# When the weight difference for S7 is taken, and who reads A11's sum first

## The chip, the cores and the metric

The kernel runs on one core of a Trainium2 chip. The metric is the device time of one execution in microseconds (us), the median of several runs. The engines are TensorE (PE, its weight loads PEld), VectorE (DVE), ScalarE (ACT), GpSimd (POOL) and SyncE (SP), which issues the DMA transfers here. They run at their own pace and wait for each other through semaphores; each works through its own queue in order.

## What is computed

Two layers of a transformer-like backbone run on 128 context tokens and 512 latent tokens at once (640 columns), with the same weights. Each layer is: a modulated RMSNorm and a half-step SwiGLU FFN, a token-mixing stage, and a second such FFN. The change touches the FFNs alone:

```python
D_MODEL = 1024; D_FF = 2816; DEPTH = 2; SEQ = 128; DEC_SEQ = 512

def swiglu(h, wi, wo):
    a, b = jnp.split(h @ wi, 2, axis=-1)
    return (jax.nn.silu(a) * b) @ wo

def trunk_layer(x, mod, ...):
    h = mod_norm(x, norm_g[0], mod, 0)
    x = x + 0.5 * mod[..., 2, :] * swiglu(h, ffn1_wi, ffn1_wo)
    ...                                # token mixing
    h = mod_norm(x, norm_g[2], mod, 2)
    x = x + 0.5 * mod[..., 8, :] * swiglu(h, ffn2_wi, ffn2_wo)
```

All is float32. The modulation `mod` (adaLN) is a product of the conditioning with its own weights; the kernel computes it in short bursts on TensorE between other work.

## The kernel before

**Precision.** A float32 product is made of three passes. Weights and data are each split into a high part (rounded to the format TensorE takes, `fp32r`) and a low part (what is left); the passes are high x high, low x high and high x low. The weights come as raw float32 tiles by DMA. For each weight block ScalarE writes the high part (line 256, `wt<-raw`) and GpSimd the low part (line 257, which reads the raw block and the high part). I call the two together a conversion; they are made by `w_split`, one block after the other in the order of a list that `ffn_convs` writes out.

**Seven products for eight.** The first product of an FFN, `h @ wi`, is cut into 22 blocks of 128 columns of `a` and of `b`. For one block the weights are two raw tiles of 128x1024, each seen as two halves of 128x512: `r[0]` holds A11 and A12, `r[1]` holds A21 and A22. The 640 tokens are cut in two halves of 320. The 2x2 product of blocks is made with seven products instead of eight (the scheme of Strassen and Winograd). Each is 12 matmuls of 128x320. Their order in a block, with the weights, and the bank of PSUM that each adds to, is

- S2 (A21+A22, bank D), S5 (A11+A12, bank C), A22 (bank D again), A11 (bank C again), S1 (A11+A22, bank A), S6 (A21-A11, bank E), S7 (A12-A22, bank A again).

The data operands are named B (for S2 and S5), X (A22 and S1), P (A11, S7) and Q (S6 and the last pass of S7). So in the views one product is a row `ps<-X,wt x12`, and S7 is a row of 8 with P and one of 4 with Q; A11 is the row with P x12.

**Sums and differences of weights.** They are VectorE operations of 128x512, all recorded on line 121 (`into`). Each is the `prep` of an entry of the list: `s2` writes the sum for S2 to `sq`; `s5` writes the sum for S5 to `acc` and calls `s7`, the difference for S7, which is written in place (`raw<-raw`); `s6`, the difference for S6, also in place, belongs to A22; `s1` writes the sum for S1 to `t`. `w_split` takes the prep of the next entry as soon as it has issued a conversion, and an entry whose prep was issued in one step of the program (`self.now`, one per product) is converted in a later step at the earliest. An entry without a prep may follow at once. Which step is reached when, and so the place of every conversion among the other instructions, is thus set by the list, by the number of weight slots that are free (`wcap`) and by the calls of `pump` after each product.

**What is done with the products.** `step` reads the banks. After S2, ScalarE copies bank D to `b` (line 844). After S5, VectorE adds bank C to it (line 851). After A22, `gate_a` reads bank D and `b` (line 869). After A11, ScalarE takes the silu of bank C into the first half of `a` (line 859), and VectorE adds bank C to the first half of `b` or subtracts (line 860). Line 860 also adds bank A to `b` after S1 and bank E after S6. After S6 the first halves of `a` and `b` are multiplied (line 821); after S7 VectorE adds bank A to the second half of `a` (line 855), ScalarE takes its silu (line 856), VectorE multiplies the second halves (line 821 again), and the result is split in a high and a low part `av` (lines 828 and 829).

**Stages of an FFN.** The first four blocks are written out by hand in `first`, product by product across blocks, with their own list entries. Then the groups of `FFG` follow (4, 2, 4, 4, 4, 4 blocks; the first of these is `first`): the blocks of a group one after the other, then the part of the second product, `(...) @ wo`, that this group feeds (lines 443, 445, 447, read by line 672). Conversions for later blocks go on all the while. In some groups of the first three FFNs an adaLN burst (line 368) stands between A22 and A11.

Of the kernel before, what the change touches and what calls it, by code (L numbers as in the profile page):

```python
# [81 lines left out]
class Kernel:  # L82
# [26 lines left out]
    def ffn_convs(self, f, u0):  # L109


        nc = self.nc
        out = []

        def conv(name, j, units, src, prep=None, frees=()):
            out.append(Conv((f, name, j), units, src, prep, frees, early=name != "D" and j >= FIRST))

        q = lambda r, i: r[:, i * 512 : i * 512 + 512]

        def into(o, x, y, op=ALU.add, eng=nc.vector):  # L120
            eng.tensor_tensor(o, x, y, op=op)  # L121

        ab = lambda j: (u0 + 2 * j, u0 + 2 * j + 1)
        first = range(FIRST)
        for j in first:
            b = ab(j)[1]
            conv("S2", j, (b,), lambda r: q(r[0], 0), lambda r: into(q(r[0], 0), q(r[0], 0), q(r[0], 1)))
            conv("A22", j, (b,), lambda r: q(r[0], 1), frees=(b,))
        for j in first:
            a = ab(j)[0]  # L130
            conv("S5", j, (a,), lambda r: q(r[0], 1), lambda r: into(q(r[0], 1), q(r[0], 0), q(r[0], 1)))
            conv("A11", j, (a,), lambda r: q(r[0], 0), frees=(a,))

        def s6(r, eng=nc.vector):
            into(q(r[1], 0), q(r[1], 0), q(r[0], 0), ALU.subtract, eng)

        def s7(r, eng=nc.vector):
            into(q(r[0], 1), q(r[0], 1), q(r[1], 1), ALU.subtract, eng)

        def s2(r):  # L140
            assert not self.acc_live
            into(self.nb["sq"][:, :512], q(r[1], 0), q(r[1], 1))

        def s5(r):
            into(self.nb["acc"][:, :512], q(r[0], 0), q(r[0], 1))
            s7(r)

        def s1(r):
            into(self.nb["t"][:, :512], q(r[0], 0), q(r[1], 1))

        j0, ud = 0, u0 + 2 * NFF
        for name, j in ((name, j) for j in first for name in ("S1", "S7", "S6")):
            a, b = ab(j)
            if name == "S1":
                eng = nc.gpsimd if f == (0, 0) and ("S1", j) in ON_POOL else nc.vector
                conv("S1", j, (a, b), lambda r: q(r[0], 0), (
                    lambda r, eng=eng: s6(r, eng), lambda r, eng=eng: s7(r, eng),
                    lambda r, eng=eng: into(q(r[0], 0), q(r[0], 0), q(r[1], 1), eng=eng),
                ))
            elif name == "S7":  # L160
                conv("S7", j, (a,), lambda r: q(r[0], 1), frees=(a,))
            else:
                conv("S6", j, (b,), lambda r: q(r[0], 0), frees=(b,))
        for gi, gn in enumerate(FFG):
            for j in range(max(j0, FIRST), j0 + gn):
                a, b = ab(j)
                conv("S2", j, (a, b), lambda r: self.nb["sq"][:, :512], s2)
                conv("S5", j, (a, b), lambda r: self.nb["acc"][:, :512], s5)
                conv("A22", j, (a, b), lambda r: q(r[1], 1), s6)
                conv("A11", j, (a, b), lambda r: q(r[0], 0))  # L170
                conv("S1", j, (a, b), lambda r: self.nb["t"][:, :512], s1)
                conv("S6", j, (a, b), lambda r: q(r[1], 0), frees=(b,))
                conv("S7", j, (a,), lambda r: q(r[0], 1), frees=(a,))
            for i in range(gn * KD // 8):
                for h in range(2):
                    conv("D", (gi, 2 * i + h), (ud,), lambda r, h=h: q(r[0], h), frees=(ud,) if h else ())
                ud += 1
            j0 += gn
        return out
# [613 lines left out]
    def ffn(self, l, s, gate, nxt):  # L793
# [7 lines left out]
        half = [slice(*self.geo.half[g]) for g in range(2)]  # L801
        tt, add, sub, mul = nc.vector.tensor_tensor, ALU.add, ALU.subtract, ALU.mult
# [33 lines left out]
        def step(p, name, now=None, pump=99):  # L836


            self.now += 1
            x, acc, start = USE[name]  # L840
            bank = p[acc]
            self.prod((f, name, p["j"]), x, bank, start)
            if name == "S2":
                nc.scalar.copy(p["b"][:, half[0]], bank)
            elif name == "A22":
                if p["early"]:
                    nc.scalar.copy(p["b"][:, half[1]], bank)
                else:
                    gate_a(p)
            elif name == "S5":  # L850
                tt(p["b"][:, half[0]], p["b"][:, half[0]], bank, op=add)
                if p["early"]:
                    gate_a(p)
            elif name == "S7":
                tt(p["a"][:, half[1]], p["a"][:, half[1]], bank, op=add)
                nc.scalar.activation(p["a"][:, half[1]], p["a"][:, half[1]], AF.Silu)
            else:
                if name == "A11":
                    nc.scalar.activation(p["a"][:, half[0]], bank, AF.Silu)  # L859
                tt(p["b"][:, half[0]], bank, p["b"][:, half[0]], op=sub if p["neg"] else add)  # L860
                p["neg"] = False
            if now is not None:
                now()
            self.ada_rest()
            if pump:
                self.pump(n=pump)

        def gate_a(p):
            tt(p["a"][:, half[1]], p["D"], p["b"][:, half[0]], op=sub)

        def new(j):
            a, b = (self.tp.tile([128, PADW], F32, name=n, tag="t" + n)[:, :NT] for n in "ab")
            return {"j": j, "neg": True, "early": j < FIRST, "a": a, "b": b}

        def first():
# [6 lines left out]
            def st(name, j, now=None, pump=0):  # L882
                if name == "S2":
                    banks(ps[j], "DC")
                elif name in ("S1", "S6"):
                    banks(ps[j], "A" if name == "S1" else "E")
                step(ps[j], name, now, pump)
# [131 lines left out]
        for gi, gn in enumerate(FFG):  # L1019
            pairs = first() if gi == 0 else None  # L1020
            for j in range(FIRST if gi == 0 else j0, j0 + gn):
                p = new(j)
                if s and j == NFF - 2:
                    self.ada_stop = True
                banks(p, "CE")
                banks(p, "DA")
                step(p, "S2")
                end(1)
                step(p, "S5")
                end()  # L1030
                step(p, "A22")
                self.ada_tick()
                step(p, "A11")
                step(p, "S1")
                if l == s == 0:
                    self.ada_tick()
                step(p, "S6", lambda: gated(p, 0))
                if pairs is None:
                    pairs = av(gn)
                step(p, "S7", lambda: finish(p, pairs[j - j0]))  # L1040
# [993 lines left out]
```

## Time and profile before

| what | us |
|---|---|
| median of 3 runs | 2570.98 |
| lowest and highest run | 2566.62, 2575.92 |
| the profiled execution | 2573.96 |
| its span, first to last instruction | 2572.2 |
| TensorE busy in the span | 2378.7 |
| GpSimd busy | 1546.1 |
| VectorE busy | 1695.7 |
| ScalarE busy | 1037.5 |

The profile is one execution. Its page gives the busy time of each engine, the chain of work that ended last (followed back from the last instruction, at each step to what released it) and the costliest groups of instructions. The trace behind it answers narrower questions: who waited for whom, and the instructions of one engine in order of time in a window. In the timeline a row gives start and duration in us, engine, line, operation, output and inputs, a count of merged instructions, and in brackets the idle time of the engine ahead of it with what ended it. Matmuls overlap at their edges, so a product of 12 has a row of 1.92 us although the next starts 1.76 us after it. Times count from the start of the span.

### The profile page before, as it was taken

The page shows a single profiled execution, that of the slowest core. Times are in us where ns is not written, and L with a number is a line of the kernel's source. Part 1 is how long each engine was busy: PE and PEld are TensorE (multiplying, and loading weights), DVE is VectorE, ACT ScalarE, POOL GpSimd, SP SyncE. Part 2 cuts the span into 40 slices and gives each one's busy share as a digit, 9 for nine tenths or more (in the row PEclk, how much of TensorE's full clock was granted, in tenths as well). Part 3 has the DMA queues.
Part 4 walks back from the last instruction along what each step waited for, and adds up shares of the span by engine and source line. Part 5 has one row for each costly group of instructions (what it writes and reads, how often), then busy time and mean ns, then how long its engine had stood idle before and what let it go on. Part 6 is the DMA issues. An engine that isn't in the chain of part 4 may idle for free.

```text
span 2572.2 us, 45355 instructions
## 1 busy us (share of the span) xinstructions
PE 2378.7 (92%) x17790; PEld 2314.6 (90%) x17790; DVE 1695.7 (66%) x2931; ACT 1037.5 (40%) x2234; POOL 1546.1 (60%) x1460
## 2 busy tenths in 40 slices
PE   5699999989889899999997999999889898999999
PEld 4698999989888899999996999999889798999999
DVE  6466566667675876556666776666766767766664
ACT  5233233333664533233343333334437654343332
POOL 2565567653366575565564876667434676677663
PEclk9799999989999999999998999999989999999999
DMA  7465422231112234556231321224111032222121
GB/s 268 143 239 201 158 89 83 82 95 56 31 39 99 82 115 179 210 202 216 92 119 60 105 75 66 82 83 124 40 54 44 31 126 99 82 83 91 58 82 50
DMA packets 80484, 272.31 MB, mean 106 GB/s; under 512 B 9232, under 2 KB 15120, under 8 KB 80272
## 3 DMA queue, kind: packets, MB, share of 16 engines
q1 hardware_dynamic: 79408, 269.33, 30.8%
q8 instruction: 140, 2.29, 0.4%
q14 instruction: 72, 0.59, 0.1%
q10 hardware_dynamic: 864, 0.10, 0.0%
HBM read 265.73 MB, written 3.67 MB: 105 GB/s over the span
## 4 chain that ended last, share of the span: by engine, by line
PE 68%; DVE 16%; issue 5%; ACT 4%; POOL 4%; DMA 2%; SPq 0%; POOLq 0%; ACTq 0%; DVEq 0%
PE ps L787 29%; PE ps L443 9%; PE ps L445 9%; PE ps L447 9%; DVE raw L121 3%; PE ada L368 2%; POOL wt L257 2%; DVE acc L121 1%; DVE b L860 1%; DVE t L121 1%; PE qk L1262 1%; PE qk L1263 1%; PE qk L1261 1%; POOL win L1115 1%; DMA raw<-in_w 1%
## 5 line engine op out<-in xcount | busy, mean ns | idle before, releaser
L257 POOL TENSOR_TENSOR wt<-raw,wt 128x512 fp32r<-128x512 f32 (+1 forms) x562 | 902.2, 1622 | 501.8 <-ACT wt L256 500.8
L443 PE MATMUL ps<-av,wt 128*128 128x320 f32 (+2 forms) x1536 | 477.7, 312 | 0.1
L447 PE MATMUL ps<-av,wt 128*128 128x320 f32 (+2 forms) x1536 | 474.2, 310 | 0.0
L256 ACT ACTIVATE wt<-raw 128x512 fp32r<-128x512 f32 (+1 forms) x562 | 350.7, 659 | 294.2 <-issue 149.1
L445 PE MATMUL ps<-av,wt 128*128 128x320 f32 (+2 forms) x1536 | 460.4, 311 | 0.0
L672 DVE SCALAR_TENSOR_TENSOR x<-ps,modv,x 128x512 f32<-128x512 f32 (+3 forms) x496 | 231.5, 512 | 267.4 <-PE ps L447 198.7
L787 PE MATMUL ps<-X,wt 128*128 128x320 f32 x2112 | 346.1, 314 | 28.4 <-DVE b L860 8.1
L787 PE MATMUL ps<-B,wt 128*128 128x320 f32 x2112 | 339.9, 317 | 32.7 <-POOL wt L257 13.1
L787 PEld LDWEIGHTS ps<-B,wt 128*128 128x128 f32 x2112 | 323.7, 194 | 38.2 <-POOL wt L257 16.0
L787 PEld LDWEIGHTS ps<-X,wt 128*128 128x128 f32 x2112 | 319.0, 190 | 35.9 <-DVE b L860 8.3
L787 PE MATMUL ps<-P,wt 128*128 128x320 f32 x1760 | 298.1, 318 | 30.7 <-DVE b L860 24.5
L787 PEld LDWEIGHTS ps<-P,wt 128*128 128x128 f32 x1760 | 269.6, 193 | 44.4 <-DVE b L860 25.0
L443 PEld LDWEIGHTS ps<-av,wt 128*128 128x128 f32 x1536 | 290.4, 189 | 1.9 <-issue 0.8
L447 PEld LDWEIGHTS ps<-av,wt 128*128 128x128 f32 x1536 | 290.1, 189 | 0.0
L445 PEld LDWEIGHTS ps<-av,wt 128*128 128x128 f32 x1536 | 285.8, 189 | 1.6 <-issue 1.4
L860 DVE TENSOR_TENSOR b<-ps,b 128x320 f32<-128x320 f32 x240 | 116.8, 487 | 201.8 <-ACT a L859 129.7
L787 PE MATMUL ps<-Q,wt 128*128 128x320 f32 x1408 | 237.5, 312 | 0.0
L121 DVE TENSOR_TENSOR raw<-raw 128x512 f32<-128x512 f32 x181 | 208.2, 1155 | 13.8 <-DMA raw<-in_w 8.7
L787 PEld LDWEIGHTS ps<-Q,wt 128*128 128x128 f32 x1408 | 216.6, 190 | 0.2 <-DVE t L821 0.2
L257 POOL TENSOR_TENSOR wt<-t,wt 128x512 fp32r<-128x512 f32 x72 | 93.7, 1301 | 130.6 <-ACT wt L256 92.7
L257 POOL TENSOR_TENSOR wt<-acc,wt 128x512 fp32r<-128x512 f32 x72 | 112.9, 1569 | 64.9 <-ACT wt L256 64.9
L257 POOL TENSOR_TENSOR wt<-sq,wt 128x512 fp32r<-128x512 f32 x72 | 112.3, 1560 | 60.4 <-ACT wt L256 60.4
(275 smaller groups left out, 4027.4 us busy)
## 6 DMA issues: line engine op xcount, KB each, us to landing
raw<-in_w SPq DMA_DIRECT2D x311, 512.0 KB, 3.5
ada<-in_adat SPq DMA_DIRECT2D x40, 1024.0 KB, 7.5
ada<-in_adat SPq DMA_DIRECT2D x64, 512.0 KB, 6.5
scraw<-in_w SPq DMA_DIRECT2D x33, 512.0 KB, 3.8
x<-in_xt SPq DMA_DIRECT2D x2, 1280.0 KB, 7.8
out_yt<-x SPq DMA_DIRECT2D x16, 160.0 KB, 1.8
dft<-in_dft SPq DMA_DIRECT2D x4, 512.0 KB, 4.0
kqv<-in_inv SPq DMA_DIRECT2D x4, 336.0 KB, 4.5
```

What stands on the lines that cost most here:

```text
L121: eng.tensor_tensor(o, x, y, op=op)
L256: nc.scalar.activation(hi, src, AF.Copy)
L257: nc.gpsimd.tensor_tensor(lo, src, hi.bitcast(F32), op=ALU.subtract)
L368: nc.tensor.matmul(ps[32 * q : 32 * q + 32, 0, :128], self.scP[:, k, :], units[q // parts][:, k * 128 : k * 128 + 128], start=(i == 0), st ...
L443: mm(out, w[0], x[0], start=start, stop=False)
L445: mm(out, w[0], x[1], start=False, stop=part == 1 and stop)
L447: mm(out, w[1], x[0], start=False, stop=part is None and stop)
L672: self.nc.vector.scalar_tensor_tensor(out=self.x[:, d, c0:c1], in0=ps[:, c0 - o : c1 - o], scalar=self.mod(l, s, d, cond), in1=self.x[:, d ...
L787: mm(out, w[:, k * 128 : k * 128 + 128], v[:, k * 320 : k * 320 + 320], start=start and i == k == 0, stop=i == 2 and k == 3, skip_group_ch ...
L860: tt(p["b"][:, half[0]], bank, p["b"][:, half[0]], op=sub if p["neg"] else add)
L1115: steps.append(lambda: nc.gpsimd.tensor_tensor(out(), a(), b(), op=op))
L1261: mm(ps[:, 0, :256], h0, wk[:, 0, :], start=(k == 0), stop=False)
```

## The change

It has two parts. The difference for S7 is no longer taken with the prep of S5 but becomes the prep of A11, in the list for blocks from the fifth on. And in `step`, for A11, the instruction of VectorE that adds bank C to `b` stands ahead of ScalarE's silu of the same bank; this part holds for the first four blocks of each FFN too.

```diff
         def s5(r):
             into(self.nb["acc"][:, :512], q(r[0], 0), q(r[0], 1))
-            s7(r)
...
-                conv("A11", j, (a, b), lambda r: q(r[0], 0))
+                conv("A11", j, (a, b), lambda r: q(r[0], 0), s7)
...
             else:
+                tt(p["b"][:, half[0]], bank, p["b"][:, half[0]], op=sub if p["neg"] else add)
+                p["neg"] = False
                 if name == "A11":
                     nc.scalar.activation(p["a"][:, half[0]], bank, AF.Silu)
-                tt(p["b"][:, half[0]], bank, p["b"][:, half[0]], op=sub if p["neg"] else add)
-                p["neg"] = False
```

In the changed file lines from 146 on count one less; line 860 has become 857, and line 859 has become 860. The number of instructions is the same on every engine, and TensorE, GpSimd and SyncE have the same instructions in the same order.

VectorE, the end of the first block of a group of four and the start of the second, before (`t<-raw` is the sum for S1):

```order
L860 TENSOR_TENSOR b<-ps,b 128x320
L821 TENSOR_TENSOR b<-a,b 128x320
L121 TENSOR_TENSOR t<-raw 128x512
L855 TENSOR_TENSOR a<-a,ps 128x320
L821 TENSOR_TENSOR b<-a,ps 128x320
L851 TENSOR_TENSOR b<-b,ps 128x320
L829 TENSOR_TENSOR av<-b,av 128x640
```

and now:

```order
L857 TENSOR_TENSOR b<-ps,b 128x320
L820 TENSOR_TENSOR b<-a,b 128x320
L121 TENSOR_TENSOR raw<-raw 128x512
L854 TENSOR_TENSOR a<-a,ps 128x320
L820 TENSOR_TENSOR b<-a,ps 128x320
L121 TENSOR_TENSOR t<-raw 128x512
L850 TENSOR_TENSOR b<-b,ps 128x320
L828 TENSOR_TENSOR av<-b,av 128x640
```

The difference (`raw<-raw`) has taken the place of `t` ahead of S7's sum (line 855, now 854), and `t` has gone behind the product of the second halves, ahead of the next block's sum for S5 (line 851, now 850).

VectorE, the second block of that group, from the high and low split of the first block's result (line 829) on, before:

```order
L829 TENSOR_TENSOR av<-b,av 128x640
L869 TENSOR_TENSOR a<-ps,b 128x320
L121 TENSOR_TENSOR sq<-raw 128x512
L860 TENSOR_TENSOR b<-ps,b 128x320
L121 TENSOR_TENSOR acc<-raw 128x512
L121 TENSOR_TENSOR raw<-raw 128x512
L860 TENSOR_TENSOR b<-ps,b 128x320
L121 TENSOR_TENSOR raw<-raw 128x512
L860 TENSOR_TENSOR b<-ps,b 128x320
L821 TENSOR_TENSOR b<-a,b 128x320
L855 TENSOR_TENSOR a<-a,ps 128x320
L821 TENSOR_TENSOR b<-a,ps 128x320
```

and now:

```order
L828 TENSOR_TENSOR av<-b,av 128x640
L868 TENSOR_TENSOR a<-ps,b 128x320
L121 TENSOR_TENSOR sq<-raw 128x512
L857 TENSOR_TENSOR b<-ps,b 128x320
L121 TENSOR_TENSOR acc<-raw 128x512
L857 TENSOR_TENSOR b<-ps,b 128x320
L121 TENSOR_TENSOR raw<-raw 128x512
L857 TENSOR_TENSOR b<-ps,b 128x320
L820 TENSOR_TENSOR b<-a,b 128x320
L121 TENSOR_TENSOR raw<-raw 128x512
L854 TENSOR_TENSOR a<-a,ps 128x320
L820 TENSOR_TENSOR b<-a,ps 128x320
```

Behind `acc` one difference is gone, so that S1's sum follows it; the difference now stands behind the product of the first halves (line 821, now 820), ahead of S7's sum (line 855, now 854).

ScalarE, the same turn from the first to the second block, from the silu of A11 on, before (`wt<-...` are high parts of weights):

```order
L859 ACTIVATE a<-ps 128x320
L256 ACTIVATE wt<-sq 128x512
L256 ACTIVATE wt<-acc 128x512
L256 ACTIVATE wt<-raw 128x512 x2
L856 ACTIVATE a<-a 128x320
L844 COPY b<-ps 128x320
L256 ACTIVATE wt<-t 128x512
L256 ACTIVATE wt<-raw 128x512
```

and now:

```order
L860 ACTIVATE a<-ps 128x320
L255 ACTIVATE wt<-sq 128x512
L255 ACTIVATE wt<-acc 128x512
L255 ACTIVATE wt<-raw 128x512
L855 ACTIVATE a<-a 128x320
L255 ACTIVATE wt<-raw 128x512
L843 COPY b<-ps 128x320
L255 ACTIVATE wt<-t 128x512
L255 ACTIVATE wt<-raw 128x512
```

The last conversion of the four, that of A11, has moved from ahead of S7's silu (line 856, now 855) to behind it, and so ahead of the copy of S2's bank (line 844, now 843).

## Rows read from the trace of the kernel before

**Rows 1.** The page: busy time and share of each engine; the chain by engine.

```profile
PE 2378.7 (92%) x17790; PEld 2314.6 (90%) x17790; DVE 1695.7 (66%) x2931; ACT 1037.5 (40%) x2234; POOL 1546.1 (60%) x1460
...
PE 68%; DVE 16%; issue 5%; ACT 4%; POOL 4%; DMA 2%; SPq 0%; POOLq 0%; ACTq 0%; DVEq 0%
```

**Rows 2.** Waits of TensorE and VectorE: who for whom, us in total, times, longest.

```profile
PE ps L787 <- DVE b L860: 32.6, 35, 8.1
...
PE ps L787 <- DVE t L860: 6.2, 3, 2.5
...
PE ps L787 <- DVE a L869: 4.5, 3, 1.5
...
DVE b L860 <- ACT a L859: 129.7, 63, 7.9
```

**Rows 3.** Timeline of TensorE in a plain group of four blocks.

```profile
1579.94 1.92 PE L787 MATMUL ps<-X,wt 128*128 128x320 f32 x12
1581.70 1.92 PE L787 MATMUL ps<-P,wt 128*128 128x320 f32 x12
...
1587.37 1.43 PE L787 MATMUL ps<-P,wt 128*128 128x320 f32 x8 [0.23 <-DVE b L860]
...
1593.10 2.02 PE L787 MATMUL ps<-X,wt 128*128 128x320 f32 x12 [0.18 <-ACT b L844]
...
1601.20 1.45 PE L787 MATMUL ps<-P,wt 128*128 128x320 f32 x8 [0.81 <-DVE b L860]
...
1606.60 1.92 PE L787 MATMUL ps<-X,wt 128*128 128x320 f32 x12
```

**Rows 4.** Timeline of VectorE in the same group.

```profile
1584.13 0.49 DVE L860 TENSOR_TENSOR b<-ps,b 128x320 f32<-128x320 f32 x1 [1.74 <-ACT a L859]
...
1585.26 1.66 DVE L121 TENSOR_TENSOR raw<-raw 128x512 f32<-128x512 f32 x1
1586.84 0.48 DVE L860 TENSOR_TENSOR b<-ps,b 128x320 f32<-128x320 f32 x1
...
1590.05 1.78 DVE L121 TENSOR_TENSOR t<-raw 128x512 f32<-128x512 f32 x1
...
1603.86 0.47 DVE L855 TENSOR_TENSOR a<-a,ps 128x320 f32<-128x320 f32 x1
...
1605.28 0.68 DVE L121 TENSOR_TENSOR t<-raw 128x512 f32<-128x512 f32 x1
```

**Rows 5.** Timeline of ScalarE in the same group.

```profile
1583.66 0.44 ACT L859 ACTIVATE a<-ps 128x320 f32<-128x320 f32 x1 [2.30 <-PE ps L787]
...
1592.64 0.41 ACT L844 COPY b<-ps 128x320 f32<-128x320 f32 x1
```

**Rows 6.** Timeline of GpSimd in the same group.

```profile
1584.70 1.67 POOL L257 TENSOR_TENSOR wt<-sq,wt 128x512 fp32r<-128x512 f32 x1 [0.47 <-ACT wt L256]
...
1593.65 1.29 POOL L257 TENSOR_TENSOR wt<-t,wt 128x512 fp32r<-128x512 f32 x1 [2.37 <-DVE b L851]
```

**Rows 7.** Timeline of TensorE in a group with adaLN bursts.

```profile
1187.24 1.44 PE L787 MATMUL ps<-P,wt 128*128 128x320 f32 x8 [0.61 <-DVE b L860]
...
1202.88 1.44 PE L787 MATMUL ps<-P,wt 128*128 128x320 f32 x8 [0.27 <-DVE b L860]
```

**Rows 8.** Timeline of TensorE, the sixth block of the second FFN.

```profile
964.85 2.02 PE L787 MATMUL ps<-X,wt 128*128 128x320 f32 x12 [1.51 <-DVE a L869]
```

**Rows 9.** Timeline of TensorE, then VectorE, first four blocks of the second FFN.

```profile
888.69 2.47 PE L787 MATMUL ps<-P,wt 128*128 128x320 f32 x8 [3.98 <-DVE b L860]
...
905.08 2.12 PE L787 MATMUL ps<-P,wt 128*128 128x320 f32 x8 [2.41 <-DVE t L860]
...
884.59 0.49 DVE L860 TENSOR_TENSOR b<-ps,b 128x320 f32<-128x320 f32 x1 [2.16 <-ACT a L859]
...
900.40 0.49 DVE L860 TENSOR_TENSOR sq<-ps,sq 128x320 f32<-128x320 f32 x1 [2.23 <-ACT acc L859]
```

**Rows 10.** Windows: us, busy of each engine, PEclk the granted clock, DMA share, GB/s.

```profile
888.40:891.80 3.40, 3.11 (x12) 3.14 (x13) 2.64 (x4) 1.48 (x3) 1.91 (x2) 0.50 0.46 157
```

## The prediction

> **What bounds the kernel now.** I read the busy table and the chain first. TensorE is busy 92% of a span of 2572.2 us and holds 68% of the chain that ended last; VectorE comes second with 16% [rows 1]. So time can be won only where TensorE stands still, and the view of waits says for whom it does: 35 times, 32.6 us in all, for the sum of line 860 into `b`, three times for the same sum into `t` (6.2 us), three times for line 869 (4.5 us) [rows 2]. Line 860 itself has stood idle 129.7 us until ScalarE's silu of line 859 was done [rows 2]; most of that is idle time of an engine that is not the bottleneck.
>
> The timeline shows where the 35 waits are. From the third weight group on, each FFN has groups of four blocks; the program has 16 of them, 12 plain and 4 in which adaLN bursts stand between the products. In a plain one products follow each other every 1.76 us (1579.94, 1581.70), so 14 of them need 24.64 us; from the first block's A22 (1579.94) to the third's (1606.60) it is 26.66 [rows 3]. The 2.02 us are lost at three places: S7 of the first block (0.23 idle), A22 of the second (0.18), S7 of the second (0.81); each stop costs 0.1 to 0.3 more than its idle time, because the products no longer overlap at their edges. The reason on VectorE: S7 adds to the bank that line 860 reads after S1, and that sum (1586.84) stands behind the difference for S7 (1585.26, 1.66 us), which stands behind A11's sum (1584.13), which waits for the silu [rows 4]. A22 waits for ScalarE's copy of line 844 (1592.64, done 1593.05) [rows 5].
>
> A second thing is to be read there. The same difference `t` takes 1.78 us at 1590.05 and 0.68 at 1605.28 [rows 4]: in the first case GpSimd was in the middle of a conversion. GpSimd's operation is 1.29 alone [rows 6]. Where GpSimd is busy, a VectorE operation with two SBUF inputs ends about 0.55 us after GpSimd's: the difference of 1585.26 ends at 1586.92, GpSimd's operation of 1584.70 at 1586.37 [rows 4, 6]. GpSimd's next one then runs its 1.2 or 1.3. Sums that read PSUM stay at 0.49 [rows 4].
>
> **The change, part by part.** No instruction is added or taken away; TensorE, GpSimd and the DMA queue keep their order.
>
> (1) *The swap.* VectorE's A11 sum starts when TensorE is done and not 0.47 us later (1584.13 against the silu's start, 1583.66) [rows 4, 5]. The silu gets the wait instead: it starts 0.49 us later, and ScalarE's conversions for S2 and S5 are queued behind it. In a plain group GpSimd, which waits for them, stands idle for 0.47 us ahead of the first of them and for 2.37 us before the next `t` [rows 6], so I cost this at nothing; without that pause it is 0.49 per block. The silu's reader, line 821, comes two products later.
>
> (2) *The difference moved.* In the first block S1's sum follows `acc` directly, is there 1 us before S7 needs it, and the stop is gone: 0.49 us, its 0.23 idle and 0.26 at the edges (the 2.02 less the three idle times, 1.22, shared out to three stops). The difference now stands ahead of S7's own sum (line 855) in place of `t`, and `t` goes behind the silu of S7. Worked from the rows: A11's sum ends at 1584.15, `acc` 1584.8, S1's sum 1585.9, S6's difference 1587.1, S6's sum 1587.7, line 821 1588.6, S7's difference 1590.3, line 855 1590.7, silu 1591.2. A11's conversion is now between silu and copy (the order of ScalarE below), 0.62 us: the copy ends at 1592.05, in time for A22 at 1592.27. Second stop gone, 0.44 us.
>
> (3) *The second block pays.* `t` (0.68, GpSimd idle then) is new in it, and line 829 now meets GpSimd (about 0.5 longer). A11's sum runs at 1597.0, `acc` ends at 1598.8, S1's sum at 1599.2: S7 starts without a stop at 1599.4. But both differences remain ahead of line 855: S6's to 1600.5, S6's sum, line 821 to 1602.0, S7's to 1603.7, line 855 to 1604.1 (before: 1603.86 to 1604.33), silu 1604.6, conversion, copy to 1605.5. TensorE is ready for the third block's A22 at 1604.65, so a new stop of 0.9 us stands there: A22 at 1605.5 instead of 1606.60. Then the third block's S1 waits some 0.3 us for line 869, which stands behind a late 829. Net 0.8 us for a plain group. Bounds: 2.0, if the contention falls out well and nothing is new; minus 0.6, if S6's difference, line 821 and S7's difference each meet a whole GpSimd operation (three times 0.5 later than in my walk). I take 0.8, the walk with each duration from the nearest row: 12 x 0.8 = 9.6 us.
>
> What the Trainium skill says (SBUF — State Buffer, Who interferes with whom): the engine that comes first keeps the shared SBUF ports for its whole instruction and the other waits fully. By that rule alone a difference could cost 1.29 + 0.68 = 1.97 us, and with 1.97 for the two in the second block a plain group would keep only some 0.3 us, the sum 6 us less. The longest row here is 1.78, and I go by the rows.
>
> (4) *Groups with bursts.* They stop at the same three places, 0.61 and 0.27 idle ahead of S7 [rows 7], some 1.9 us in all with the edges. The burst gives VectorE 2 us between A22 and A11, which takes up the lateness of (3): I take 1.7, bounds 0.9 and 1.9. 4 x 1.7 = 6.8 us.
>
> (5) *Sixth block of three FFNs.* S1 waits 1.51 us for line 869 [rows 8], behind both differences. One of them goes behind it, but line 829 now meets GpSimd's operation elsewhere and S7 gets a small stop: 0.6 each (0 to 1.7), 1.8 us.
>
> (6) *First four blocks of each FFN.* Here ScalarE is far behind at A11. In the second FFN the sum stood 2.16 us idle for the silu and S7 stopped for 3.98; later 2.23 and 2.41 [rows 9]. With the swap the first sum runs 2.16 us earlier, and what is queued behind it moves up by about as much, S7 too; but the next S1 then waits for its weights, so I count 1.6. The other place gives 1.0, since line 829, next on VectorE, has to wait for ScalarE anyway. Behind the stop of 3.98 the first eight matmuls took 2.47 us against 1.43 in a plain group [rows 3, 9], since the granted clock was at its lower level there, 0.50 of full speed or 1.2 GHz [rows 10]; whether the shorter stop leaves it up I leave to the upper bound. 2.6 for this FFN and the fourth, which has the same stops; for the first and third, where conversions and DMA set the pace, 1.1. Sum 7.4 us, bounds 0 and 12.
>
> Total: 9.6 + 6.8 + 1.8 + 7.4 = 25.6 us. The span goes from 2572.2 to 2546.6, the profiled execution from 2573.96 to 2548.4. That execution lies 3 us above the median of the runs (2570.98), so the median goes to about 2545.4 to 2548; I say 2547.
>
> **The rivals.** A difference under 0.3% (7.7 us: 2563.3 to 2578.7) can hardly be told from no change here.
>
> *The second block eats it (same time).* Both differences stand ahead of line 855, which gates silu, copy and A22. For: the moved work is not less, and in my walk line 855 is already at its old time. Against: the first block's two stops have no such queue. Plain groups give 0.0, the sixth blocks and half of (6) nothing: 6.8 + 3.7 = 10.5, less 3 for edges: 2563 to 2567.
>
> *It turns over (slower).* If each VectorE operation of the second block meets a full GpSimd operation, line 855 comes 1.5 us after its old time against TensorE, A22 of the third block stops for 2.1, and its S1 for 0.8 because line 869 is late: minus 1.1 per plain group, minus 0.3 with bursts, nothing from (6): 12 x 1.1 + 4 x 0.3 = 14.4 us, 2585. It decides from line 855 being over 1.2 us later than in the walk. Against: GpSimd stands idle for 2.37 us in the second block [rows 6].
>
> *The swap does nothing.* Both engines read the same bank, and one must wait for the other; the Trainium skill (PSUM — Partial Sum Buffer, PSUM bank collisions raise a hardware error) asks for that order, ScalarE against VectorE too. If the silu is what others wait for, (6) turns to 0, which leaves 18.2 us, and 0.49 us comes back in each block where GpSimd has no pause; with up to 20 such blocks that is 2553 to 2563.
>
> *Everything goes.* No new stop in the third block (12 x 2.0), 4 x 1.9, 1.5 x 3 and 10 from the first blocks: 46 us, 2525.
>
> **How the numbers follow.** My forecast 58%; everything goes 10%; the second block eats it 18%; the swap does nothing 5%; slower 9%. Faster by over 0.3%: 55 of the first, 10, 6 of the third, 4 of the fourth, 75%. Within 0.3%: 3 + 12 + 1 = 16%. Slower by over 0.3%: 9%. The range of 8 in 10 leaves out the best ends (below 2530) and the slower case with some of the equal one (above 2568).
>
> **What would show it.** Right: in plain groups the stops before S7 are gone and line 860 no longer heads the waits of TensorE; a stop of about 0.9 us for line 844 stands before the third block's A22. The silu of line 859 (860 after) waits for VectorE, by about half a microsecond. In the first blocks the stops of 3.98 and 2.41 shrink to near 2 and 1.2. Wrong: line 855 of the second block more than 0.6 us from 1604.1 on the scale above; stops for GpSimd's conversions where none were; S7's stop of the second block still above 0.3.

## The result, and the profile after

| what | us |
|---|---|
| median of 4 runs, before | 2570.76 (2566.62 to 2575.92) |
| median of 4 runs, changed | 2544.40 (2541.45 to 2548.60) |
| ratio | 0.990, 95% interval 0.9883 to 0.9917 |
| the profiled execution of the changed kernel, its span | 2541.77, 2540.0 |

The change takes 26.4 us off; 24 had been forecast (2547), and the time lies in the range. The two profiled executions differ by 32.2 us, because that of before lies 3.2 us above the median of its runs and that of after 2.6 below. Stages are compared in the traces below, totals by the medians.

The page of the changed kernel, busy time and the chain by engine [rows 1]:

```profile
PE 2375.3 (94%) x17790; PEld 2311.2 (91%) x17790; DVE 1667.8 (66%) x2931; ACT 1036.1 (41%) x2234; POOL 1527.0 (60%) x1460
...
PE 67%; DVE 15%; issue 6%; ACT 5%; POOL 4%; DMA 1%; DVEq 0%; ACTq 0%; POOLq 0%; SPq 0%
```

TensorE works as long as before in a span that is 32 us shorter. Its view of waits (who for whom, us in total, times, longest) has lost the head that it had in [rows 2]:

```profile
DVE b L857 <- PE ps L786: 190.7, 160, 9.7
ACT a L860 <- DVE b L857: 176.2, 76, 7.8
...
PEld ps L786 <- ACT a L860: 13.5, 16, 7.3
...
PE ps L786 <- ACT a L860: 7.1, 1, 7.1
...
PEld ps L786 <- DVE a L868: 6.3, 28, 0.3
...
PE ps L786 <- DVE t L857: 4.7, 2, 2.3
...
PE ps L786 <- DVE b L857: 2.6, 2, 1.3
...
PE ps L786 <- ACT b L843: 2.0, 12, 0.2
```

The sum into `b` (860, now 857) made TensorE wait 35 times for 32.6 us; now it is twice, 2.6 us. Not all of that is gained: the longest of the 35, 8.1 us in the first FFN, is still there with 7.1, and now ends with the silu. The waits have changed hands as the order says: 857 waits for TensorE, the silu (now 860) for VectorE. Two kinds of small waits of the weight loads are new, 28 of up to 0.3 us for line 868 and 15 of 0.4 for the silu. The 12 stops for the copy (line 843) stood in the plain groups before too (line 844), but ahead of the second block's A22; now it is the third's. Timeline of TensorE in the same plain group as [rows 3] (start, duration, and in brackets the idle time ahead), then of its weight loads at the two places where the product started late without an idle time in the first view:

```profile
1558.62 1.92 PE L786 MATMUL ps<-X,wt 128*128 128x320 f32 x12
...
1563.90 1.92 PE L786 MATMUL ps<-Q,wt 128*128 128x320 f32 x12
1565.66 1.34 PE L786 MATMUL ps<-P,wt 128*128 128x320 f32 x8
...
1570.94 1.92 PE L786 MATMUL ps<-X,wt 128*128 128x320 f32 x12
1572.70 1.92 PE L786 MATMUL ps<-P,wt 128*128 128x320 f32 x12
1574.54 2.02 PE L786 MATMUL ps<-X,wt 128*128 128x320 f32 x12
1576.71 2.02 PE L786 MATMUL ps<-Q,wt 128*128 128x320 f32 x12
1578.57 1.34 PE L786 MATMUL ps<-P,wt 128*128 128x320 f32 x8
...
1584.18 2.03 PE L786 MATMUL ps<-X,wt 128*128 128x320 f32 x12 [0.17 <-ACT b L843]
```

```profile
1574.54 1.76 PEld L786 LDWEIGHTS ps<-X,wt 128*128 128x128 f32 x12 [0.17 <-DVE a L868]
1576.70 0.44 PEld L786 LDWEIGHTS ps<-Q,wt 128*128 128x128 f32 x3 [0.41 <-ACT a L860]
```

From the first block's A22 to the third's it is now 25.56 us (1558.62 to 1584.18) for 26.66. The three old stops are gone: S7 follows S6 by 1.76 in the first block, A22 follows its S5 in step, and in the second block S7 follows S6 by 1.86. In their place S1 of the second block is 0.08 late (it waits for 868), S6 0.41 (for the silu), and A22 of the third block has a stop of 0.17. VectorE and ScalarE there [rows 4, 5]:

```profile
1572.83 1.25 DVE L828 TENSOR_TENSOR av<-b,av 128x640 fp32r<-128x640 f32 x1 [1.13 <-ACT av L827]
...
1575.70 0.48 DVE L857 TENSOR_TENSOR b<-ps,b 128x320 f32<-128x320 f32 x1
...
1580.61 1.78 DVE L121 TENSOR_TENSOR raw<-raw 128x512 f32<-128x512 f32 x1
1582.32 0.47 DVE L854 TENSOR_TENSOR a<-a,ps 128x320 f32<-128x320 f32 x1
```

```profile
1576.21 0.44 ACT L860 ACTIVATE a<-ps 128x320 f32<-128x320 f32 x1 [2.62 <-DVE b L857]
...
1583.72 0.41 ACT L843 COPY b<-ps 128x320 f32<-128x320 f32 x1
```

From 828 to 854 VectorE has no pause of over 0.1 us: that chain now sets the pace. The silu at 1576.21 has to follow the sum of 1575.70, and S6, whose bank lies in one tile with A11's, waits for both.

### The profile page after: what moved, and what is told of

The parts are those of the page before. It is cut to its first block, busy times and chain, and to the rows that moved or that the text cites. A ratio compares the mean times of both kernels' runs of the same rounds, so it can differ in the third digit from the quotient of the medians.

```text
span 2540.0 us, 45467 instructions
## 1 busy us (share of the span) xinstructions
PE 2375.3 (94%) x17790; PEld 2311.2 (91%) x17790; DVE 1667.8 (66%) x2931; ACT 1036.1 (41%) x2234; POOL 1527.0 (60%) x1460
## 3 DMA queue, kind: packets, MB, share of 16 engines
HBM read 265.73 MB, written 3.67 MB: 106 GB/s over the span
## 4 chain that ended last, share of the span: by engine, by line
PE 67%; DVE 15%; issue 6%; ACT 5%; POOL 4%; DMA 1%; DVEq 0%; ACTq 0%; POOLq 0%; SPq 0%
PE ps L786 29%; PE ps L442 9%; PE ps L446 9%; PE ps L444 9%; DVE raw L121 3%; PE ada L367 2%; POOL wt L256 2%; ACT wt L255 1%; DVE b L820 1%; DVE b L857 1%; POOL win L1114 1%; DMA ada<-in_adat 1%; DVE t L549 1%; PE qk L1261 1%; PE qk L1262 1%
## 5 line engine op out<-in xcount | busy, mean ns | idle before, releaser
L786 PE MATMUL ps<-P,wt 128*128 128x320 f32 x1760 | 292.6, 314 | 7.3 <-DVE t L857 4.7
L121 DVE TENSOR_TENSOR raw<-raw 128x512 f32<-128x512 f32 x181 | 200.8, 1114 | 10.8 <-DMA raw<-in_w 8.9
L256 POOL TENSOR_TENSOR wt<-sq,wt 128x512 fp32r<-128x512 f32 x72 | 99.1, 1376 | 71.4 <-ACT wt L255 71.4
```

Source lines behind the costliest of these rows:

```text
L256: nc.gpsimd.tensor_tensor(lo, src, hi.bitcast(F32), op=ALU.subtract)
L786: mm(out, w[:, k * 128 : k * 128 + 128], v[:, k * 320 : k * 320 + 320], start=start and i == k == 0, stop=i == 2 and k == 3, skip_group_ch ...
```

## Where the time went, stage by stage

The stages repeat so exactly (plain groups of one kernel agree to 0.05 us) that they tell more than the totals. The table gives, from the timeline of TensorE, the time from the start of the first matmul of a stage's products to the start of the last one; "down" is what follows up to the next products. E1 to E12 are the experiments of the next section.

| stage | before | changed | E1 | E2 | E3 | E4 | E5 | E6 | E7 | E11 | E12 |
|---|---|---|---|---|---|---|---|---|---|---|---|
| a plain group (12 of them) | 51.15 | 50.41 | 49.77 | 50.30 | 50.31 | 50.42 | 49.77 | 49.77 | 49.26 | 49.77 | 49.26 |
| three groups with bursts, second FFN | 179.7 | 173.7 | 173.7 | 175.4 | 175.3 | 174.6 | 173.7 | 173.7 | 175.1 | 173.7 | 173.7 |
| down behind these three | 95.7 | 99.0 | 96.2 | 103.9 | 99.0 | 100.5 | 95.7 | 95.8 | 96.0 | 95.9 | 95.8 |
| fifth and sixth block (FFN 2 to 4, each) | 26.44 | 25.21 | 26.88 | 24.74 | 24.76 | 25.21 | 26.89 | 26.44 | 26.10 | 25.21 | 26.09 |
| first four blocks, sum of four FFNs | 319.7 | 307.4 | 309.0 | 315.0 | 308.0 | 315.7 | 306.1 | 304.0 | 305.6 | 305.8 | 309.0 |

The last row differs by some us between executions of one kind, since there TensorE stops for up to 8 us and its granted clock may or may not fall behind such a stop. E2, whose first blocks have the order of before, is 4.7 us shorter there than before: 2.5 in the third FFN, from places where the clock or a late weight differ, and 1.6 in the second, where a stop of 2.95 us for a weight stands in both, but the eight matmuls behind it take 2.46 us before and 1.44 in E2. So of the 12.3 us between before and changed in this row only a part is the swap's (E4). From the fifth block on there is nothing of that kind.

## The experiments

**E1: the swap alone.**

```diff
 the kernel before, with
-                if name == "A11":
-                    nc.scalar.activation(p["a"][:, half[0]], bank, AF.Silu)
                 tt(p["b"][:, half[0]], bank, p["b"][:, half[0]], op=sub if p["neg"] else add)
                 p["neg"] = False
+                if name == "A11":
+                    nc.scalar.activation(p["a"][:, half[0]], bank, AF.Silu)
```

> The kernel before with the swap alone; the difference for S7 stays with S5's prep. Theory A (the swap wins the first four blocks of each FFN, the moved difference wins the later groups): the first four blocks give about 9 us, the plain groups at most the first block's stop of 0.23 idle, since VectorE is 0.47 us earlier there, and part of the second's 0.81: 12 x 0.5 to 1.0; in all 14 to 20 us, 2551 to 2557 us. Rival B (half a microsecond on VectorE is all that the later groups lacked, from wherever it comes): plain groups 12 x 1.2, groups with bursts 4 x 1.3, first blocks 9: about 29 us, 2542 us, no slower than both parts together. Rival C (the swap is worth nothing, readers of one bank wait for each other either way): 2568 to 2573 us.

2540.63 us, ratio 0.9885 (0.987 to 0.990). Rival B holds, against the account of the prediction: the swap alone gives all that both parts give. Its plain group is even 0.64 us shorter than that of the changed kernel. One stop of the three is left (timeline of TensorE, then of VectorE and of GpSimd, in the same group):

```profile
1577.88 1.44 PE L787 MATMUL ps<-P,wt 128*128 128x320 f32 x8 [0.37 <-DVE b L858]
```

```profile
1562.11 0.70 DVE L121 TENSOR_TENSOR acc<-raw 128x512 f32<-128x512 f32 x1
1562.84 0.69 DVE L121 TENSOR_TENSOR raw<-raw 128x512 f32<-128x512 f32 x1
1563.46 0.49 DVE L858 TENSOR_TENSOR b<-ps,b 128x320 f32<-128x320 f32 x1
...
1571.37 0.89 DVE L829 TENSOR_TENSOR av<-b,av 128x640 fp32r<-128x640 f32 x1 [0.31 <-ACT av L828]
```

```profile
1563.26 1.44 POOL L257 TENSOR_TENSOR wt<-sq,wt 128x512 fp32r<-128x512 f32 x1 [1.00 <-ACT wt L256]
```

Before, the difference for S7 took 1.66 us in this place, because GpSimd had begun a conversion 0.56 us ahead of it [rows 4, 6]. The swap brings VectorE forward by 0.47 and puts ScalarE's conversion, and with it GpSimd's, back: GpSimd now starts at 1563.26, 0.42 us behind the difference, which takes 0.69. So half a microsecond in the order of two readers gives back a whole one. In the sixth block, where the move helps, E1 is 0.44 us slower than before.

**E2: the moved difference alone.**

```diff
 the changed kernel, with
+                if name == "A11":
+                    nc.scalar.activation(p["a"][:, half[0]], bank, AF.Silu)
                 tt(p["b"][:, half[0]], bank, p["b"][:, half[0]], op=sub if p["neg"] else add)
                 p["neg"] = False
-                if name == "A11":
-                    nc.scalar.activation(p["a"][:, half[0]], bank, AF.Silu)
```

> The changed kernel with ScalarE's silu ahead of VectorE's sum again; the difference for S7 stays at A11's prep. Theory A: nothing in the first four blocks of an FFN; in plain groups the two stops ahead of S7 go, and S6 no longer waits 0.41 us for the silu: 0.8 to 1.2 each, groups with bursts 1.9, sixth blocks 1.05: 12 x 1.0 + 4 x 1.9 + 3 x 1.05 = 23 us at most, 17 at least: 2548 to 2554 us. Rival B (VectorE's half microsecond is what counts): without the swap line 855 of the second block is late by another 0.47, plain groups give 0.2 and the whole about 12 us: 2559 us.

2556.74 us, ratio 0.9952 (0.994 to 0.9965): 13.8 us, between the two expectations. A plain group gives what theory A says (0.85), a sixth block more (1.7) and a group with bursts less (1.4), but 8.1 us come back in the down parts of the table, 5.3 of them behind one group of this execution. There the moved difference has pushed `t` into the down part. ScalarE, then VectorE, then TensorE of the changed kernel, behind its first group with bursts in the second FFN:

```profile
1046.04 0.63 ACT L255 ACTIVATE wt<-t 128x512 fp32r<-128x512 f32 x1 [8.05 <-DVE t L121]
1046.57 0.61 ACT L255 ACTIVATE wt<-raw 128x512 fp32r<-128x512 f32 x1
1047.09 0.24 ACT L372 COPY arow<-ada 128x128 f32<-128x128 f32 x1
```

```profile
1048.09 1.20 DVE L399 TENSOR_SCALAR modv<-modv 128x4 f32<-128x4 f32 x1
```

```profile
1047.39 0.33 PE L381 MATMUL ada<-ident,arow 128*128 128x128 f32 x1 [0.45 <-ACT arow L372]
...
1059.26 1.94 PE L367 MATMUL ada<-ada,scP 128*32 128x128 f32 x58 [0.63 <-DMA ada<-in_adat]
```

Two conversions, held up by `t`, stand ahead of the burst's copy (0.45 us of TensorE). GpSimd's part of the second, and then SyncE's next load of a raw tile, which waits for it; last the same load in E1:

```profile
1047.98 1.29 POOL L256 TENSOR_TENSOR wt<-raw,wt 128x512 fp32r<-128x512 f32 x1
```

```profile
1049.30 0.33 SPq L208 DMA_DIRECT2D raw<-in_w  x1
```

```profile
1048.54 0.33 SPq L209 DMA_DIRECT2D raw<-in_w  x1
```

The next burst's weights are behind that load in SyncE's queue, so against the burst ahead of the copy (at 1044.50 here, 1045.12 in E1) they are fetched 1.4 us later than in E1, and TensorE waits 0.63 for them. The 128x4 operation takes 1.20 us beside the same conversion, where E1's takes 0.17; that it delays TensorE is not shown. All four kernels with the difference moved in every later block and GpSimd's reads in place have all of this; of the others only E9 below has the copy's stop, and none the rest.

**E3 and E4: both parts, the swap only in the first four blocks of each FFN (E3), or only from the fifth on (E4).** E3 (E4 has `not p["early"]` in both places):

```diff
-                if name == "A11":
+                if name == "A11" and not (p["early"]):
+                    nc.scalar.activation(p["a"][:, half[0]], bank, AF.Silu)
+                tt(p["b"][:, half[0]], bank, p["b"][:, half[0]], op=sub if p["neg"] else add)
+                p["neg"] = False
+                if name == "A11" and p["early"]:
                     nc.scalar.activation(p["a"][:, half[0]], bank, AF.Silu)
```

> Both parts, but the swap only in the first four blocks of each FFN. In the changed kernel S6 of a plain group's second block waits 0.41 us for the silu that the swap put behind VectorE's sum (15 such places, 6 us). Theory 1 (that wait is a true price): without it the kernel is 5 to 6 us faster than the changed one, 2538.5 us. Theory 2 (VectorE is busy without a pause from line 828 to line 854 there, so the time comes back as a longer stop ahead of the third block's A22): the same as the changed kernel within 2 us, 2543 to 2546 us.

2544.10 us, ratio 0.9902 (0.9887 to 0.9918), the same as the changed kernel: theory 2. S6's wait for the silu is gone, and the stop ahead of the third block's A22 is 0.59 for 0.17 (waits, who for whom):

```profile
PE ps L786 <- ACT b L843: 7.2, 12, 0.6
```

The wait of 0.41 was no price of its own; VectorE's chain sets the end of the second block either way. So with the difference moved the swap is worth nothing in a plain group (50.31 and 50.41), though alone it is worth 1.38.

> Both parts, but the swap only from the fifth block of each FFN on. The difference to the changed kernel is what the swap gives in the first four blocks. By the places of the two profiled executions that is 8 to 11 us (3.8, 4.3 and 2.8 in the second to fourth FFN, part of it in the granted clock): 2552.5 to 2555.5 us. By the term of the prediction, 7.4 us: 2552 us. Rival (most of it was the clock of one execution): 2 to 4 us, 2546.5 to 2548.5 us.

2556.55 us, ratio 0.9954 (0.9941 to 0.9968). Against the changed kernel, which differs from it in the first four blocks alone, the swap there is worth about 12 us by the medians and 8.4 by that row of the table (1.2, 2.8, 1.6 and 2.8 us in the four FFNs); the rest is in down parts with bursts and in scatter. That is within, by the medians 1 us beyond, the 8 to 11 expected. The rival (2 to 4 us) is out.

**E5, E6 and E11: the swap everywhere, the move only where it helps.** E5, with `gn == 2` for the fifth and sixth block; E6 is E5 with the silu ahead of the sum in these two; E11 has `j == 6`, the seventh, in both places:

```diff
 the changed kernel, with
-                conv("S5", j, (a, b), lambda r: self.nb["acc"][:, :512], s5)
+                conv("S5", j, (a, b), lambda r: self.nb["acc"][:, :512], s5 if gn == 2 else (s5, s7))
...
-                conv("A11", j, (a, b), lambda r: q(r[0], 0), s7)
+                conv("A11", j, (a, b), lambda r: q(r[0], 0), s7 if gn == 2 else None)
```

> The swap everywhere; the difference for S7 at A11's prep only in the fifth and sixth block of each FFN, at S5's prep in all later ones. Theory (a stage keeps the time that it has with either kernel): the plain groups stay at the 49.77 us of the swap alone (50.41 with both parts), the group of two blocks gets the 25.20 us of both parts (26.88 with the swap alone), 3 x 1.68 and 0.2 in the first FFN: 5.2 us less than the swap alone, 2535.4 us. Rival (the queues of one stage carry into the next, so that the times don't add): 2538 to 2544 us.

> As e5, but with the silu ahead of the sum in the fifth and sixth block. Their group took 24.73 us with the move alone and 25.20 with both: 3 x 0.46 us less than e5, 2534 us; the plain groups stay at 49.77. Rival (carried into the next stage): no difference to e5 within 1 us, with the plain group behind it longer by what this one gained.

E5: 2537.92 us (2530.36 to 2546.38), ratio 0.9883 (0.9862 to 0.9904). The plain groups stay, but the fifth and sixth block take 26.89 us and not 25.20: the move had no effect at all where it was to help. E6: 2534.18 us, ratio 0.987 (0.9857 to 0.9884); the total was met, the reason not: its two blocks take the 26.44 us of before, as without a move. The list runs a block ahead. What VectorE takes during the sixth block is the seventh's, and that one was left at S5. E11 tests this:

> As e5, but with the difference for S7 moved for the seventh block of each FFN alone, since the sums and differences that VectorE takes during the sixth block belong to the seventh. Theory: the group of two blocks takes 25.20 us (26.88 with the swap alone), the plain groups stay at 49.77; 3 x 1.68 us less than the swap alone (2540.6): 2535.5 us. Rival (e5 missed for another reason): the group of two stays at 26.88 us, 2540 us.

2534.98 us, ratio 0.9864 (0.9848 to 0.9881); fifth and sixth block 25.21 us, plain groups 49.77, as the theory has it. VectorE in the sixth block of the second FFN, E5 and then E11:

```profile
947.94 0.69 DVE L121 TENSOR_TENSOR acc<-raw 128x512 f32<-128x512 f32 x1
948.66 1.67 DVE L121 TENSOR_TENSOR raw<-raw,scraw 128x512 f32<-128x512 f32 x1
...
950.65 1.38 DVE L121 TENSOR_TENSOR scraw<-scraw,raw 128x512 f32<-128x512 f32 x1
951.96 1.90 DVE L828 TENSOR_TENSOR av<-b,av 128x640 fp32r<-128x640 f32 x1
```

```profile
946.73 0.68 DVE L121 TENSOR_TENSOR acc<-raw 128x512 f32<-128x512 f32 x1
...
948.37 0.76 DVE L121 TENSOR_TENSOR scraw<-scraw,raw 128x512 f32<-128x512 f32 x1
949.05 1.91 DVE L828 TENSOR_TENSOR av<-b,av 128x640 fp32r<-128x640 f32 x1
```

From `acc` to 828 it is 4.02 us in E5 and 2.32 in E11; the 1.70 are the whole difference of the stage.

**E7 and E12: the rounding of line 828 earlier.** E7 is the swap alone with this, E12 is E11 with it:

```diff
-                step(p, "S2")
-                end(1)
+                step(p, "S2", lambda: end(1))
```

> The swap alone, and the end of the block before (ScalarE's rounding of line 828, on which VectorE's line 829 waits) ahead of the conversions that follow S2, not behind them. In the swap alone line 829 of a plain group's second block starts at 1571.37, right behind 828, and VectorE has almost no pause until S7's stop of 0.38 us. Theory (the chain from 829 on sets that stop): 829 is 0.7 to 1.1 us earlier, the stop goes, a plain group takes 49.2 us for 49.77, and the S1 of the sixth block waits 0.7 instead of 1.5 for line 869: 12 x 0.55 + 3 x 0.8 = 9 us, 2531.5 us. Rival (the conversion for S1, now 0.7 us later, is itself late, or the moved operations meet GpSimd's elsewhere): 2538 to 2546 us.

2530.19 us (2529.97 to 2530.45), ratio 0.9854 (0.984 to 0.9867): the theory, a little better. A plain group takes 49.26 us, and the stop ahead of S7 in the second block is gone. Line 829 starts 0.67 us behind A22 (1567.98 to 1567.31) for 1.07 in E1, so only 0.4 earlier, but the sum behind it now lies otherwise to GpSimd's work and takes 0.83 us for 1.30.

> e11 with the early rounding of e7. Theory (the places don't disturb each other): plain groups 49.26 us as in e7, the group of two between 24.5 and 25.2 us for 26.10: 3 x 0.9 to 1.6 us less than e7 (2530.2), 2525.4 to 2527.5 us. Rival (the seventh block's start pays for it): the group behind it is longer by as much, 2530 us.

2531.38 us, ratio 0.9844 (0.9829 to 0.9859): no better than E7, and the places do disturb each other. That is the rival's time without its reason, since no group behind is longer than in E7. The fifth and sixth block stay at 26.09: the rounding, put ahead of the conversion of `sq`, lets GpSimd start on it 0.96 us later against A22 (0.49 behind it, 948.40 to 947.91, for 0.47 ahead of it, 947.22 to 947.69), and the difference that took 0.76 in E11 now runs beside it (VectorE of E12):

```profile
948.59 1.65 DVE L121 TENSOR_TENSOR scraw<-scraw,raw 128x512 f32<-128x512 f32 x1
```

E7, E11 and E12 beat both kernels of this case, with 0.9854, 0.9864 and 0.9844 of before against 0.990.

**E8, E9, E10: GpSimd without its reads.** In the kernel before (E8), the changed one (E9) and the swap alone (E10):

```diff
-        nc.gpsimd.tensor_tensor(lo, src, hi.bitcast(F32), op=ALU.subtract)
+        nc.gpsimd.memset(lo.bitcast(F32), 0.0)
```

> The kernel before, with GpSimd's low parts of the weights left out: GpSimd writes zeros in their place and reads nothing. Read in the plain groups alone (51.15 us from the first matmul of their products to the last). Theory (the stops come from VectorE operations that meet a GpSimd operation: 1.2 to 1.8 us for 0.68): the differences take 0.7 us, a plain group has no stops, 49.1 to 49.4 us. Rival (VectorE's wait for the silu makes them by itself): at least 50.2 us, the stop ahead of S7 in the second block stays.

> The changed kernel with the same left out. Theory (contention): its plain group, 50.41 us, comes to the 49.1 to 49.4 of the kernel before, so that the change is worth nothing there. Rival (queue order): it stays shorter than the kernel before by 0.5 us or more.

> The swap alone with the same left out. Theory (contention): 49.1 to 49.4 us for a plain group, as in the other two; the 0.63 us by which it beats both parts together are a matter of which VectorE operation meets GpSimd's. Rival (queue order): it stays shorter than both parts by 0.3 us or more.

A plain group takes 49.13 us in all three, the fifth and sixth block 24.49, the groups with bursts of the second FFN 57.91: these stages have no stop left, and neither part of the change is worth anything there (2447.6, 2448.9 and 2443.6 us in all, one run each). The theory of contention holds. In a plain group of E8 the third block's A22 starts 24.64 us behind the first's, just 14 products of 1.76:

```profile
1498.61 1.92 PE L787 MATMUL ps<-X,wt 128*128 128x320 f32 x12
...
1523.25 1.92 PE L787 MATMUL ps<-X,wt 128*128 128x320 f32 x12
```

The sums and differences of E8 (line 121, count, then min/median/max of one in ns):

```profile
L121 DVE TENSOR_TENSOR raw<-raw x181: 678/683/1210, 26.9 to 2374.8; 128x512 f32<-128x512 f32 x181
...
L121 DVE TENSOR_TENSOR t<-raw x62: 678/683/689, 131.6 to 2376.6; 128x512 f32<-128x512 f32 x62
```

In the kernel before, the medians of the same two were 1.36 and 1.67 us. Of the 434 VectorE operations of line 121 in E8, 210 run beside a GpSimd operation that writes zeros, and none of them takes over 0.70 us; the only ones above that, up to 1.21, are among the eight beside a GpSimd sum of line 508, which still reads. VectorE waits for the silu as it did (E8 has the order of before), and yet TensorE has no stop in these stages. One reserve: the zeros are also written faster, 0.53 us for 1.55, and wait for no high part; but weights were not what a plain group waited for. What the swap gives in the first four blocks stays: in the second and fourth FFN 2.7 us each between E8 and E9 (56.74 and 54.03, 56.73 and 54.04), and in E10, with the swap alone, 2.7 and 2.0. That part is queue order. In the first FFN the two are longer than E8 instead, by 2.6 and 3.0 us (86.70 in E8), in single runs; why is open. The down parts behind the groups with bursts are 2.2 us longer in E9 than in E8: most of what the move costs there is queue order too.

## Why the prediction was right, and where it wasn't

**The total** was right: 2547 forecast, 2544.4 measured. By stages its four terms (plain groups, groups with bursts with the down parts behind them in the second FFN, sixth blocks, first blocks) come to 8.8, 4.9, 3.7 and 8.4 us, 25.8 together for 25.6; that the second falls short by as much as the third gains is luck. The reason given for the largest term was not right.

**(1) The swap, costed at nothing in the later groups.** This is the step that failed. Alone it is worth 1.38 us in each plain group and 2.0 in one with bursts. The working looked for what it would delay and didn't ask what VectorE does with the 0.47 us: get a difference done before GpSimd starts (E1). The walk does take A11's sum at its early time, so its 0.8 is the value of both parts together. The working also left out that S6 waits for the silu; E3 shows that this costs nothing beside VectorE's chain.

**(2), (3) The move.** The size and the places were right: 0.74 us a plain group for 0.8. In the walk line 855 began 11.4 us behind the second block's A22, and the third A22 13.2; both are measured at 11.38 and 13.24, and from A22 to A22 the walk gave 25.56, as measured. The stop forecast at 0.9 us is there, but 0.6 of it falls ahead of S1, S6 and S7, and 0.17 of idle time is left for line 843. What fails is the credit: the swap alone takes the same stops, and with it in place the move costs 0.64 us a plain group (E1) and gains only around the sixth block (1.68 us each) and 1.0 us in the first FFN's group with bursts.

**The rule on the SBUF ports.** The longest of VectorE's sums and differences in the changed kernel takes 1.80 us; 1.97, the sum of the two durations, does not appear here either. E8 bears on another sentence of the Trainium skill (SBUF — State Buffer, Who interferes with whom): a VectorE instruction with two SBUF inputs contends with a GpSimd one that reads SBUF, not with one that only writes it. This trace agrees: 0.68 us at the median with GpSimd writing zeros, 1.36 to 1.67 with it reading.

**(4) Groups with bursts.** 2.0 us each in the second FFN and 2.2 in the first for 1.7, but 3.3 of the second FFN's 6 us go again in the down parts behind them; the prediction stopped at the end of the products and missed that the move pushes `t` into what follows.

**(5) Sixth blocks.** 1.23 each for 0.6: line 829 did meet GpSimd (1.92 us), but the whole of one difference was gained ahead of it.

**(6) First four blocks.** 7.4 forecast; E4 against the changed kernel gives 8.4 by stages, 1.2, 2.8, 1.6 and 2.8 for 1.1, 2.6, 1.1 and 2.6 (the first and third scatter by about a microsecond: E3, with the same first blocks as the changed kernel, has 104.05 and 77.04 for 102.82 and 77.76). The places differ from the text. In the second FFN the first stop went from 3.98 to 1.29 (2 was forecast), with a wait of 1.02 for S1's weight behind it, as the text has it. The second went from 2.41 only to 2.34 (1.2 was forecast), since three differences stand ahead of that sum, and they now take 3.67 us for 2.59. TensorE there [rows 9], and the granted clock behind the second stop [rows 10]:

```profile
878.09 1.41 PE L786 MATMUL ps<-P,wt 128*128 128x320 f32 x8 [1.29 <-DVE b L857]
...
881.82 1.43 PE L786 MATMUL ps<-X,wt 128*128 128x320 f32 x8 [1.02 <-POOL wt L256]
...
894.39 2.47 PE L786 MATMUL ps<-P,wt 128*128 128x320 f32 x8 [2.34 <-DVE t L857]
```

```profile
894.10:897.50 3.40, 3.11 (x12) 3.14 (x13) 2.08 (x4) 2.70 (x6) 2.92 (x3) 0.52 0.54 158
```

Behind the shorter stop the first eight matmuls take 1.41 us, with 1.00 granted from 878 to 881, full clock (2.4 GHz); behind the one of 2.34 they take 2.47, with 0.52 granted, near its lower level (1.2 GHz). What the prediction left to the upper bound came true for the one and not for the other.

**The rivals.** That the swap does nothing is refuted by E1 and E4. That the second block eats the gain holds in part: both parts together leave 0.74 us of the 1.38 that the swap alone gives a plain group. No plain group turned slower in any run; only the sixth block of E1 and E5 did, by 0.44 us.

## What to carry to other kernels

When VectorE and GpSimd both read SBUF, an operation's cost depends on whether the other engine is in the middle of something, so a reordering by half a microsecond can be worth a whole one, or nothing beside another reordering: test the parts of a change apart, and read stages that repeat, not totals. Follow a moved operation into the stage behind the one that it was moved for. And where preparation runs a block ahead, ask which block an operation belongs to before changing it for one place.

## What the runs showed of the hardware

GpSimd's writes alone do not slow VectorE's sums (0.68 us at the median, 210 of them at most 0.70, E8), while beside its reads the medians of two of them are double and more (1.36 and 1.67 us). Not expected was that a VectorE operation of 128x4 takes 1.20 us beside GpSimd's conversion for 0.17 without. A conversion that ends 1.4 us later reaches TensorE through SyncE's queue: the transfer that waits for it holds up those behind it, and TensorE waits 0.63 us for one of these.
